# Fewer, larger transfers in a hybrid encoder layer on one core

## The chip, the core and the metric

The kernel runs on one core of a Trainium2 chip. Its time is the time on the device in microseconds (us), the median of several runs. A core has a matrix engine (TensorE, PE in the profile; its weight loads are PEld), VectorE (DVE), ScalarE (ACT), GpSimd (POOL) and SyncE (SP). Nearly every DMA of this kernel is issued from SP's queue, in one fixed order. An instruction of that queue that has to wait holds up all that stand behind it. 16 DMA engines carry the bytes.

## The reference

One layer works on two sequences, of 2048 and of 512 tokens, with 1024 channels:

```python
h = rms_norm(x, norm_w)
proj = h @ w_in                       # split into the inputs of four mixers
y_a = sgu(a_u, a_v) * silu(a_z)       # gating within chunks of 128 tokens
y_b = deltanet(b_q, b_k, b_v, b_beta, b_alpha) * silu(b_z)   # forward and backward
y_c = attention(c_q, c_k, c_v) * silu(c_z)   # 4 query heads, 2 key heads, QK norm, axial rope
y_d = pool(d_x) * silu(d_z)           # centred means of 2, 4, 8 and 16 tokens
y = x + concat(y_a, y_b, y_c, y_d) @ w_out
```

The DeltaNet is computed in chunks of 64 tokens: a unit lower triangular matrix of each chunk is inverted, and a recurrence carries a 64 x 64 state per head from chunk to chunk, once in each direction.

## The kernel before

The 2560 tokens are five blocks of 512 (`b`), or twenty tiles of 128 (`t`). Most matrix products run in fp16 on a high and a low part: three products stand for one in fp32.

- **Phase 1** (`phase1`, L200) loads x, normalises it, splits it into two halves in fp16 and stores the result `xs` to DRAM (L292, 2 MB a block). It computes the DeltaNet's q, k and v with their convolution (`conv`, L295, which stores keys and queries to `KX` and keys and values to `KV`) and the token-major inputs (`tmajor`).
- **Phase 2** (`phase2`, L564) runs three times, as three passes over other columns of `w_in`. For each block it loads `xs` again in eight pieces of 256 KB, one for each eighth `k` of the channels (`load_xs`, L737), into eight buffers. Each of the pass's products goes through `k` = 0 to 7 with three matmuls for each. A buffer comes free after the last product of the block has used its `k`. Weights arrive in columns of 128 (`split_w`, L101, and `weights`, L535): of each row of the weight matrix a piece of 512 B is read.
- **DeltaNet.** `pre(t)` (L1078) builds decay matrices and key products of one tile. It stores the four diagonal 32 x 32 blocks of every matrix to `DG`, once per direction (L1128), in pieces of 128 B, and the attention-like matrix to `AT` (L1132). A small product `ctp` with a copy `ct` (L1085 to L1090) prepares four tiles at once, when `t % 4 == 0`. `lanes` (L1135) loads the diagonal blocks of a whole block (L1145), inverts them on DVE and stores the inverses to `XL`. `levels(t)` (L1167) loads the inverses of two tiles in four transfers (L1179), joins them to inverses of 64 x 64 on PE, and stores these to `TT` (L1245). `rec(t, d, seq)` (L1256) is one step of the recurrence. It loads `kx`, `kv`, `at` and `tt`, 256 KB each (L1259 to L1265), into two buffers for each name. There are 40 such steps.
- **Phase 3** (`phase3`, L848) loads keys block by block (`load_kv`, L990: for one key head and block two transfers into `ka` and one into `kb`, 64 KB each), runs the attention with the row maxima one head ahead, and uses the output projection (`outproj`, L941) as filler on PE.

Inside `pre`, the tiles `ctp`, `gp` and `kk` take turns in the two PSUM banks of group `B` (four banks for the first block). Two allocations later the same bank is needed again, so it must have been read by then.

A planner (`schedule_with_timeline_sim`) orders each engine's instructions ahead of the run: by priorities (the DeltaNet's is above phase 2's, the attention's between) and by its own estimate of durations, transfers included. Other transfers can thus give another order on every engine.

Of the kernel before, what the change touches and what calls it, by code (L numbers as in the profile page):

```python
# [44 lines left out]
class Trunk:  # L45
# [55 lines left out]
    def split_w(self, pool, src, cols, tag, stage=None):  # L101
        nc = self.nc
        t = pool.tile([128, 2, 8, cols], F16, tag=tag, name=tag)
        for c in range(0, cols, 128):
            n = min(128, cols - c)
            w = self.stage() if stage is None else stage
            nc.sync.dma_start(w[:, :, :n], src[:, c:c + n].rearrange("(k p) c -> p k c", p=128))
            self.split_w_sb(t[:, :, :, c:c + n], w[:, :, :n])
        return t
# [13 lines left out]
    def mm_parts(self, ps, w, x):  # L123
        for k in range(8):
            for i, (a, b) in enumerate(((0, 0), (1, 0), (0, 1))):
                xk = x[k][:, b, :] if isinstance(x, list) else x[:, b, k, :]
                mm = self.nc.tensor.matmul(ps, w[:, a, k, :], xk, start=k + i == 0, stop=k == 7 and i == 2)  # L127
            yield mm.ins
# [11 lines left out]
    def consts(self, ctx):  # L140
# [8 lines left out]
        self.XS = [d.tile([128, 2, 8, 512], F16, name=f"xs{b}") for b in range(NB)]  # L149
        self.KX = [d.tile([4, 3, 64, 4, 2, 128], F16, name=f"kx{b}") for b in range(NB)]  # L150
        self.KV = [d.tile([4, 128, 512], F32, name=f"kv{b}") for b in range(NB)]
# [4 lines left out]
        self.AT = [[d.tile([128, 2, 512], F16, name=f"at{t}_{i}") for i in range(2)] for t in range(NT)]  # L156
        self.SZ = [[d.tile([128, 512], F32, name=f"sz{b}_{f}") for f in range(4)] for b in range(NB)]
        self.QS = [d.tile([2, 4, 64, 512], F16, name=f"qs{b}") for b in range(NB)]
        self.KS = [d.tile([2, 2, 64, 512], F16, name=f"ks{b}") for b in range(NB)]
        self.TT = [[d.tile([128, 2, 512], F16, name=f"tt{t}_{i}") for i in range(2)] for t in range(NT)]  # L160
# [39 lines left out]
    def phase1(self):  # L200
# [3 lines left out]
        with ExitStack() as ctx:  # L204
# [5 lines left out]
            def get_w(c, stage=None):  # L210
                if c not in W:
                    if c == "tm":
                        W[c] = self.split_w(wp, I["wtm"], 400, "wtm")
                    else:
                        W[c] = self.split_w(wp, I["wg1"][:, c * 128:(c + 1) * 128], 128, f"w1_{c}", stage)
                return W[c]
# [19 lines left out]
            def load_x(b):  # L236
# [47 lines left out]
                xs = (ho if b % 2 else he).tile([128, 2, 8, 512], F16, tag="xs", name="xs")  # L284
                for k in range(8):
                    stt = V.scalar_tensor_tensor(xt[k], xt[k], self.nw[:, k:k + 1], rb,
                                                 op0=ALU.mult, op1=ALU.mult)
                    act = A.activation(xs[:, 0, k, :], xt[k], AF.Copy)  # L288
                    if k == 3:
                        C["stt"], C["act"] = stt.ins, act.ins  # L290
                    (V if b == 0 and k % 2 else G).tensor_tensor(xs[:, 1, k, :], xt[k], xs[:, 0, k, :], op=ALU.subtract)  # L291
# [3 lines left out]
            def conv(b):  # L295
# [3 lines left out]
                for ct in range(6):  # L299
# [8 lines left out]
                    if ct < 4:  # L308
# [8 lines left out]
                        for par in range(2):  # L317
                            rows = slice(par * 64, par * 64 + 64)
                            for p in range(3):
                                nc.sync.dma_start(self.KX[b][:, p, :, par * 2 + pair, s, :].rearrange("t d f -> d t f"),  # L320
                                                  hl[rows, p % 2].rearrange("d (t f) -> d t f", t=4))
# [47 lines left out]
                nc.sync.dma_start(self.KV[b].rearrange("t p c -> p t c"), kv.rearrange("p t s h d -> p t (s h d)"))  # L369
# [18 lines left out]
            def tmajor(b, xs):  # L388
# [5 lines left out]
                for tt in range(4):  # L394
# [3 lines left out]
                    for k in range(8):  # L398
                        for a, c in ((0, 0), (0, 1), (1, 0)):
                            PE.matmul(acc[:, 0:400], xs[:, a, k, tt * 128:(tt + 1) * 128], w[:, c, k, :],  # L400
                                      start=n == 0, stop=n == 23)
                            n += 1
# [132 lines left out]
    def weights(self, *names):  # L535
# [8 lines left out]
        for n in names:  # L544
# [14 lines left out]
            if n in src:  # L559
                o, wd = src[n]  # L560
                nc.sync.dma_start(w[:, :, 0:wd], I["wg2"][:, o:o + wd].rearrange("(k p) c -> p k c", p=128))
            self.split_w_sb(self.W2[n], w)

    def phase2(self, names, ep, shared, stop=None):  # L564
# [117 lines left out]
        def store_qk(dst, s):  # L682

            if s.shape[2] == 2:
                for half in range(2):
                    for hl in range(2):
                        nc.sync.dma_start(dst[hl, :, half * 32:half * 32 + 32, :], s[:, hl, half, :])
            else:
                for half in range(2):
                    for hl in range(2):  # L690
                        nc.sync.dma_start(dst[hl, :, half * 32:half * 32 + 32, :], s[half * 64:half * 64 + 64, hl, 0, :])
# [27 lines left out]
        def finish_k(b, kt, rt):  # L719
# [6 lines left out]
            store_qk(self.KS[b], s)  # L726
# [121 lines left out]
    def phase3(self, kp, ap, wp, ep, e5, rest, post):  # L848
# [4 lines left out]
        if True:  # L853
# [136 lines left out]
            def load_kv(s0, n):  # L990
# [4 lines left out]
                for kv in range(2):  # L995
# [3 lines left out]
                    for b in range(n // 512):  # L999
                        kd = self.KS[s0 // 512 + b]  # L1000
                        c = slice(b * 512, b * 512 + 512)
                        for hl in range(2):
                            nc.sync.dma_start(ka[hl * 64:hl * 64 + 64, c], kd[hl, kv])
                        nc.sync.dma_start(kb[0:64, c], kd[0, kv])
# [63 lines left out]
    def front(self, dp, dq):  # L1068
# [9 lines left out]
        def pre(t):  # L1078
            grp = "B" if done else "B0"
            kx, ky = [dq.tile([128, 4, 2, 128], F16, tag=f"kx{i}", name="kx", bufs=2) for i in range(2)]  # L1080
            for i, x in enumerate((kx, ky)):
                nc.sync.dma_start(x.rearrange("p h s f -> p (h s f)"),
                                  self.KX[t // 4][t % 4, i:i + 2].rearrange("p d h s f -> (p d) (h s f)"))
            if t % 4 == 0:
                ctp = self.bank(grp, [128, 512], "ctp")  # L1085
                for i in range(4):
                    PE.matmul(ctp[0:24, i * 128:i * 128 + 128], self.C16[:, t + i].rearrange("p k c -> p (k c)"), self.id16,
                              start=True, stop=True)
                st["ct"] = dq.tile([24, 512], F16, tag="ct", name="ct", bufs=1)
                A.activation(st["ct"], ctp[0:24, :], AF.Copy)  # L1090
            ct = st["ct"][:, t % 4 * 128:t % 4 * 128 + 128]
# [14 lines left out]
            for par in range(2):  # L1106
# [6 lines left out]
                for d in range(2):  # L1113
# [3 lines left out]
                                           op0=ALU.mult, op1=ALU.mult)  # L1117
            for d in range(2):
                nl = nls[d]
                dg = dq.tile([128, 4, 32], F32, tag="dg", name="dg", bufs=2)  # L1120
                for B in range(4):
                    r = slice(B * 32, B * 32 + 32)
                    if d == 0:
                        V.transpose(dg[r], nl[r, :, r])
                    else:
                        A.activation(dg[r], nl[r, :, r], AF.Copy)
                l0 = (t % 4 * 2 + d) * 16
                nc.sync.dma_start(self.DG[t // 4][l0:l0 + 16].rearrange("(u b) (r c) -> (b r) u c", u=4, r=32), dg)  # L1128
# [3 lines left out]
                nc.sync.dma_start(self.AT[t][d], at)  # L1132
# [34 lines left out]
        def levels(t):  # L1167
# [5 lines left out]
            tnds = []  # L1173
            for d in both:
                TT, Tn = TTs[d], Tns[d]
                d32 = dp.tile([128, 8, 32], F32, tag=f"d32{d}", name="d32", bufs=1)
                for j in range(2):
                    l0 = ((t + j) % 4 * 2 + d) * 16
                    nc.sync.dma_start(d32[:, j * 4:j * 4 + 4], self.XL[t // 4][l0:l0 + 16].rearrange(  # L1179
                        "(u b) (c r) -> (b c) u r", u=4, c=32))  # L1180
# [57 lines left out]
            for d, Pr, Sr in ends:  # L1238
                TT = TTs[d]
                A.activation(TT[Pr, :, Sr], t2p[Pr], AF.Copy)  # L1240
                t16 = dp.tile([128, 2, 8, 128], F16, tag="tt16", name="tt16", bufs=1)
                A.activation(t16[:, 0], TT, AF.Copy)
                (G if d else V).tensor_tensor(t16[:, 1], TT, t16[:, 0], op=ALU.subtract)
                for j in range(2):
                    nc.sync.dma_start(self.TT[t + j][d], t16[:, :, j * 4:j * 4 + 4].rearrange("p i u f -> p i (u f)"))  # L1245
# [4 lines left out]
    def recurrence(self, dp):  # L1250
# [5 lines left out]
        def rec(t, d, seq):  # L1256
            b, tt = t // 4, t % 4
            kx = dp.tile([128, 4, 2, 128], F16, tag="kx3", name="kx3", bufs=2)
            nc.sync.dma_start(kx.rearrange("p h s f -> p (h s f)"),  # L1259
                              self.KX[b][tt, 0:2].rearrange("p d h s f -> (p d) (h s f)"))  # L1260
            kv = dp.tile([128, 2, 4, 64], F32, tag="kv2", name="kv2", bufs=2)
            nc.sync.dma_start(kv.rearrange("p s h d -> p (s h d)"), self.KV[b][tt])
            at, TT = [dp.tile([128, 2, 4, 128], F16, tag=n, name=n, bufs=2) for n in ("at2", "tt2")]
            nc.sync.dma_start(at.rearrange("p i u f -> p i (u f)"), self.AT[t][d])
            nc.sync.dma_start(TT.rearrange("p i u f -> p i (u f)"), self.TT[t][d])  # L1265
# [137 lines left out]
def host_arrays(np, inp):  # L1403
# [13 lines left out]
    out["wg1"] = np.concatenate([W["bq"][:, ph], W["bk"][:, ph], W["bv"][:, ph]], 1)  # L1417
    out["wtm"] = np.concatenate([W["av"], W["cv"], W["bb"], W["ba"]], 1)
# [20 lines left out]
    out["wg2"] = np.concatenate(cat, 1)  # L1439
# [46 lines left out]
```

## Time and profile before

| | us |
|---|---|
| median of 3 runs | 1571.06 (1570.57 to 1574.56) |
| the profiled execution | 1574.01 |
| its span | 1572.2 |
| PE busy | 1425.8 (91%) |
| DVE busy | 1173.3 (75%) |
| ACT busy | 797.0 (51%) |
| POOL busy | 546.7 (35%) |
| DMA, share of 16 engines | 54.1% |

The profile moves 269.65 MB in 250830 packets, 95784 of them under 512 B. Busy time of PE is the union of its instructions' times, and matmuls overlap; PE's granted clock was 0.959 of full speed in the mean. In a row of waits stand the engine and the line that waited, what it waited for, the sum in us, how often, and the longest. In a row of a timeline stand the start, the duration, the engine, the line, the instruction, how many, and in brackets the idle time before it with what ended it.

### The profile page before, as it was taken

Reading aid. Unit: us, or ns where it says so; the run is one execution under the profiler, and the core shown is the slowest. Engines: PE = TensorE matmul, PEld = TensorE weight load, DVE = VectorE, ACT = ScalarE, POOL = GpSimd, SP = SyncE. Lnnn points to the kernel's source line nnn. Section 1 sums busy time; section 2 is a strip of 40 time slices with the busy share of each in tenths; the row PEclk is TensorE's granted clock in tenths of the full one; section 3 lists DMA queues with packets and bytes.
Section 4 is the critical chain, followed back from the end, with each engine's and each line's share of the span. In section 5 each row is a group of like instructions: output and inputs, shape, how many; then the busy total and the mean of one; then the engine's idle time right before and its main releaser. Section 6 shows DMA issues by size and latency. Waiting matters only on the chain. (4 is left out here: it accounts for less than half of the span.)

```text
span 1572.2 us, 34743 instructions
## 1 busy us (share of the span) xinstructions
PE 1425.8 (91%) x13420; PEld 783.5 (50%) x13420; DVE 1173.3 (75%) x2265; ACT 797.0 (51%) x1655; POOL 546.7 (35%) x646
## 2 busy tenths in 40 slices
PE   6999999988989887987889879998799999999898
PEld 3456555543444443544445435555355555555443
DVE  6338579967969887996957769998877887877611
ACT  5244444545454844554546215565567675576400
POOL 3220220044748643455453435555121221121100
PEclk9999999998899989989999999999799999999999
DMA  9845643556566877657689885644411501414332
GB/s 254 283 168 168 190 151 114 150 194 193 160 186 201 258 234 218 199 171 215 186 259 311 278 255 177 202 139 148 161 48 39 173 34 65 160 33 135 114 128 107
DMA packets 250830, 269.65 MB, mean 172 GB/s; under 512 B 95784, under 2 KB 176680, under 8 KB 250024
## 3 DMA queue, kind: packets, MB, share of 16 engines
q1 hardware_dynamic: 250264, 267.36, 54.1%
q8 instruction: 105, 1.72, 0.4%
q14 instruction: 61, 0.50, 0.1%
q0 software_dynamic: 400, 0.07, 0.1%
HBM read 175.66 MB, written 91.77 MB: 170 GB/s over the span
## 5 line engine op out<-in xcount | busy, mean ns | idle before, releaser
L127 PEld LDWEIGHTS <-w 128*128 128x128 f16 x2280 | 223.5, 101 | 307.5 <-issue 81.8
L127 PE MATMUL accz<-xs,w 128*128 128x512 f16 x960 | 243.7, 402 | 16.8 <-DMA xs<-xs 6.7
L958 PE MATMUL op<-wo,mx 128*128 128x512 f16 x960 | 225.3, 379 | 1.0 <-DVE y L962 1.0
L886 DVE TENSOR_REDUCE mm<-mp 128x1 f32<-128x512 f32 x272 | 179.5, 683 | 52.4 <-PE mp L884 52.1
L916 POOL TENSOR_TENSOR p<-e,p 128x512 f16<-128x512 f32 x68 | 86.7, 1274 | 318.6 <-ACT p L915 283.7
L912 ACT ACTIVATE e<-sp 128x512 f32<-128x512 f32 x272 | 153.4, 596 | 79.3 <-PE sp L910 72.9
L916 DVE TENSOR_TENSOR p<-e,p 128x512 f16<-128x512 f32 x204 | 165.8, 828 | 19.3 <-ACT p L915 19.1
L127 PE MATMUL acc<-xs,w 128*128 128x512 f16 x720 | 162.8, 383 | 3.8 <-POOL xs L291 1.5
L915 ACT ACTIVATE p<-e 128x512 f16<-128x512 f32 x272 | 161.2, 632 | 3.4 <-PE O L921 2.0
L921 PEld LDWEIGHTS <-p 128*128 128x128 f16 x3264 | 128.1, 97 | 55.8 <-DVE p L916 11.2
L921 PE MATMUL O<-vt,p 128*128 128x65 f16 (+1 forms) x3264 | 142.6, 193 | 7.5 <-DVE p L916 5.3
L958 PEld LDWEIGHTS <-mx 128*128 128x128 f16 x960 | 91.3, 98 | 104.4 <-issue 1.8
L884 PE MATMUL mp<-ka,qa 128*128 128x512 f16 x272 | 98.7, 395 | 17.3 <-DVE mm L886 10.6
L909 PE MATMUL sp<-qa,ka 128*128 128x512 f16 x272 | 103.9, 384 | 2.6 <-ACT e L912 1.2
L306 DVE SCALAR_TENSOR_TENSOR cv<-raw,convw,cv 128x512 f32<-128x512 f32 x120 | 88.0, 754 | 21.2 <-POOL raw L382 20.6
L910 PE MATMUL sp<-qb,kb 65*128 65x512 f16 x272 | 100.5, 387 | 1.2 <-ACT qb L894 1.0
L127 PE MATMUL accq<-xs,w 128*128 128x512 f16 x360 | 89.5, 391 | 9.9 <-DMA xs<-xs 7.0
L400 PE MATMUL acct<-wtm,xs 128*128 128x400 f16 x480 | 83.8, 332 | 1.9 <-ACT ba L408 0.9
L1268 POOL TENSOR_TENSOR kd<-kv,kds 128x512 f16<-128x512 f32 x40 | 46.9, 1179 | 108.0 <-PE up L1305 56.0
L291 POOL TENSOR_TENSOR xs<-xt,xs 128x512 f16<-128x512 f32 x36 | 49.1, 1386 | 73.5 <-ACT xs L288 73.2
L962 DVE SCALAR_TENSOR_TENSOR y<-op,xr 128x512 f32<-128x512 f32 x40 | 27.5, 687 | 59.2 <-PE op L958 59.1
L127 PE MATMUL accu<-xs,w 128*128 128x512 f16 x240 | 60.9, 403 | 7.2 <-DVE s L616 7.0
(316 smaller groups left out, 2506.8 us busy)
## 6 DMA issues: line engine op xcount, KB each, us to landing
xs<-xs SPq DMA_DIRECT2D x120, 256.0 KB
kx<-kx SPq DMA_DIRECT2D x80, 256.0 KB
at<-at SPq DMA_DIRECT2D x80, 256.0 KB
tt<-tt SPq DMA_DIRECT2D x80, 256.0 KB
xt<-in_xT SPq DMA_DIRECT2D x40, 256.0 KB
xs<-xs SPq DMA_DIRECT2D x5, 2048.0 KB
kv<-kv SPq DMA_DIRECT2D x40, 256.0 KB
mix<-mixs SPq DMA_DIRECT2D x40, 256.0 KB
```

The source lines that it names most:

```text
L127: mm = self.nc.tensor.matmul(ps, w[:, a, k, :], xk, start=k + i == 0, stop=k == 7 and i == 2)
L306: V.scalar_tensor_tensor(cv, raw[:, ct, i:i + 512], self.convw[:, ct, i:i + 1], cv, op0=ALU.mult, op1=ALU.add)
L400: PE.matmul(acc[:, 0:400], xs[:, a, k, tt * 128:(tt + 1) * 128], w[:, c, k, :], start=n == 0, stop=n == 23)
L884: PE.matmul(mp, qa[:, qt * 128:qt * 128 + 128], KA[h // 2][:, sc * 512:sc * 512 + 512], start=True, stop=True)
L886: V.tensor_reduce(mm[:, qt, sc:sc + 1], mp, axis=AX.X, op=ALU.max)
L909: PE.matmul(sp, KA[kv][:, c], qa, start=True, stop=False)
L910: PE.matmul(sp, KB[kv][:, c], qb, start=False, stop=True)
L912: A.activation(e, sp, AF.Exp)
L915: A.activation(p[:, 0], e, AF.Copy)
L916: (G if st % E8 == 1 else V).tensor_tensor(p[:, 1], e, p[:, 0], op=ALU.subtract)
L921: mm = PE.matmul(O[:, qt, 0:z - a], p[:, w, q], v[:, a:z], start=st == 0 and qt == 0 and i == 0, stop=st == nst - 1 and i == 2, skip_group ...
L958: PE.matmul(op, mix[k][:, a, tt * 128:tt * 128 + 128], wo[k][:, c, n * 512:n * 512 + 512], start=i + j == 0, stop=i == 7 and j == 2)
```

## The change

- `xs` is stored with its halves beside each other for each `k`, and loaded in four pieces of 512 KB into four buffers (60 loads in place of 120).
- `KX` and `KV` become one tensor `KXV`, `AT` and `TT` one tensor `ATT`. A step of the recurrence loads two pieces of 512 KB in place of four of 256 KB.
- The diagonal blocks are stored once for two tiles and both directions (10 stores in place of 40), from one buffer in place of two. The inverses are loaded once for two tiles and both directions (10 in place of 40). `TT` is stored once per direction for two tiles (20 in place of 40).
- `ctp` and `ct` are made for each tile (20 in place of 5, each a quarter as wide).
- Keys are stored by sequence, and loaded in one transfer each for `ka` and `kb` (8 in place of 30).
- The host packs the weights so that a column block of 128 lies as 4 KB per partition.

```diff
+    def packed(self, w, src, o, n):
+        self.nc.sync.dma_start(w[:, :, :n], src[:, 8 * o:8 * (o + n)].rearrange("p (k c) -> p k c", k=8))
...
-            for k in range(8):
-                x = self.xp.tile([128, 2, 512], F16, tag="xs2", name="xs2", bufs=8)
-                nc.sync.dma_start(x, self.XS[b][:, :, k, :])
-                xs.append(x)
+            for k in range(0, 8, 2):
+                x = self.xp.tile([128, 2, 2, 512], F16, tag="xs2", name="xs2", bufs=4)
+                nc.sync.dma_start(x, self.XS[b][:, k:k + 2])
+                xs += [x[:, 0], x[:, 1]]
...
-                    for b in range(n // 512):
-                        kd = self.KS[s0 // 512 + b]
-                        c = slice(b * 512, b * 512 + 512)
-                        for hl in range(2):
-                            nc.sync.dma_start(ka[hl * 64:hl * 64 + 64, c], kd[hl, kv])
-                        nc.sync.dma_start(kb[0:64, c], kd[0, kv])
+                    kd = self.KS[self.seqs.index((s0, n))][kv]
+                    nc.sync.dma_start(ka, kd.rearrange("i d t -> (i d) t"))
+                    nc.sync.dma_start(kb[0:64], kd[0])
...
-            if t % 4 == 0:
-                ctp = self.bank(grp, [128, 512], "ctp")
-                for i in range(4):
-                    PE.matmul(ctp[0:24, i * 128:i * 128 + 128], self.C16[:, t + i]...
-                st["ct"] = dq.tile([24, 512], F16, tag="ct", name="ct", bufs=1)
-                A.activation(st["ct"], ctp[0:24, :], AF.Copy)
+            ctp = self.bank(grp, [128, 128], "ctp")
+            PE.matmul(ctp[0:24], self.C16[:, t].rearrange("p k c -> p (k c)"), self.id16, ...)
+            ct = dq.tile([24, 128], F16, tag="ct", name="ct", bufs=1)
+            A.activation(ct, ctp[0:24], AF.Copy)
...
+            if t % 2 == 0:
+                st["dg"] = dq.tile([128, 2, 2, 4, 32], F32, tag="dg", name="dg", bufs=1)
...
-                nc.sync.dma_start(self.DG[t // 4][l0:l0 + 16].rearrange(...), dg)
+            if t % 2:
+                l0 = t // 2 % 2 * 64
+                nc.sync.dma_start(self.DG[t // 4][l0:l0 + 64].rearrange(...), st["dg"]...)
...
-                for j in range(2):
-                    nc.sync.dma_start(d32[:, j * 4:j * 4 + 4], self.XL[t // 4][l0:l0 + 16]...
+            d32s = dp.tile([128, 2, 8, 32], F32, tag="d32", name="d32", bufs=1)
+            nc.sync.dma_start(d32s..., self.XL[t // 4][l0:l0 + 64]...)
...
-            nc.sync.dma_start(kx..., self.KX[b][tt, 0:2]...)
-            nc.sync.dma_start(kv..., self.KV[b][tt])
-            nc.sync.dma_start(at..., self.AT[t][d])
-            nc.sync.dma_start(TT..., self.TT[t][d])
+            kxv = dp.tile([128, 1024], F32, tag="kxv", name="kxv", bufs=2)
+            nc.sync.dma_start(kxv, self.KXV[b][tt, 0:128])
+            att = dp.tile([128, 2, 2, 4, 128], F16, tag="att", name="att", bufs=2)
+            nc.sync.dma_start(att..., self.ATT[t // 2][d][t % 2])
```

## Rows read from the trace of the kernel before

**Rows 1.** Windows by stretch: PE, PEld, DVE, ACT, POOL busy, PE clock, DMA share, GB/s.

```profile
320.00:480.00 160.00, 140.51 (x972) 68.68 (x969) 119.77 (x271) 84.53 (x217) 87.75 (x137) 0.90 0.58 179
480.00:640.00 160.00, 131.21 (x1442) 70.86 (x1440) 136.05 (x264) 89.43 (x213) 91.80 (x133) 0.91 0.73 225
640.00:800.00 160.00, 137.75 (x1695) 76.55 (x1696) 140.80 (x264) 82.80 (x184) 77.81 (x100) 0.91 0.66 199
800.00:960.00 160.00, 140.12 (x1622) 76.01 (x1621) 109.93 (x191) 60.93 (x121) 67.32 (x67) 0.96 0.85 271
960.00:1125.00 165.00, 145.01 (x1880) 87.07 (x1879) 147.50 (x269) 93.54 (x186) 82.21 (x79) 0.93 0.52 163
1125.00:1505.00 380.00, 368.87 (x3854) 209.39 (x3852) 289.34 (x507) 239.65 (x449) 74.88 (x56) 1.00 0.27 90
```

**Rows 2.** Waits of PE from 320 to 1120 us: sum, times, longest.

```profile
PE gp L1095 <- DVE dt L1116: 9.8, 6, 3.8
...
PE accq L127 <- DMA xs<-xs: 7.0, 8, 1.8
...
PE accz L127 <- DMA xs<-xs: 6.7, 6, 1.5
...
PE up L1300 <- DMA tt<-tt: 3.4, 2, 2.5
...
PE gp L1095 <- ACT ct L1090: 2.0, 1, 2.0
...
PE mp L884 <- DMA qa<-qs: 1.8, 1, 1.8
...
PE sp L909 <- DMA ka<-ks: 1.2, 1, 1.2
...
PE mp L884 <- DMA ka<-ks: 0.9, 1, 0.9
...
PE up L1300 <- DMA kb<-ks: 0.6, 1, 0.6
...
PE gp L1099 <- ACT ct L1090: 0.5, 1, 0.5
```

**Rows 3.** Timeline of SP's queue: the first and the last key load.

```profile
899.78 0.48 SPq L1003 DMA_DIRECT2D ka<-ks  x1
...
947.49 0.45 SPq L1004 DMA_DIRECT2D kb<-ks  x1
```

**Rows 4.** Timeline of PE in the same stretch.

```profile
907.01 4.05 PE L127 MATMUL accz<-xs,w 128*128 128x512 f16 x18
...
933.83 0.82 PE L127 MATMUL accz<-xs,w 128*128 128x512 f16 x3 [1.39 <-DMA xs<-xs]
935.96 1.41 PE L127 MATMUL accz<-xs,w 128*128 128x512 f16 x3 [1.31 <-DMA xs<-xs]
```

**Rows 5.** Issues on SP's queue by tile: duration in ns, least, median, most.

```profile
L741 SPq DMA_DIRECT2D xs<-xs x120: 517/562/2554, 47.9 to 1010.6; - x120
...
L1264 SPq DMA_DIRECT2D at<-at x40: 319/376/677, 356.8 to 1090.5; - x40
...
L1265 SPq DMA_DIRECT2D tt<-tt x40: 319/407/2168, 483.7 to 1084.2; - x40
...
L1179 SPq DMA_DIRECT2D d<-xl x40: 360/498/1196, 437.4 to 807.0; - x40
```

**Rows 6.** Windows around the first load of inverses, columns as in rows 1.

```profile
430.00:434.00 4.00, 3.88 (x10) 1.18 (x9) 1.83 (x6) 0.70 (x2) 2.04 (x12) 0.50 1.03 371
...
440.00:443.00 3.00, 3.00 (x15) 1.37 (x14) 0.00 (x0) 0.45 (x1) 1.16 (x1) 1.00 1.03 196
```

**Rows 7.** Waits of DVE for diagonal blocks and for inverses, whole span.

```profile
DVE ltmp L1153 <- DMA lnl<-dg: 20.2, 5, 7.2
...
DVE tnd L1183 <- DMA d<-xl: 10.2, 5, 4.5
```

**Rows 8.** Windows by stretch, the second 40 us, columns as in rows 1.

```profile
40.00:80.00 40.00, 37.86 (x199) 19.47 (x198) 15.93 (x33) 13.00 (x29) 10.61 (x9) 1.00 0.87 281
```

More of the change, by code (lines that the diff above doesn't have):

```diff
@@ L125, in mm_parts @@
             for i, (a, b) in enumerate(((0, 0), (1, 0), (0, 1))):
-                xk = x[k][:, b, :] if isinstance(x, list) else x[:, b, k, :]
-                mm = self.nc.tensor.matmul(ps, w[:, a, k, :], xk, start=k + i == 0, stop=k == 7 and i == 2)
+                xk = x[k] if isinstance(x, list) else x[:, k]
+                mm = self.nc.tensor.matmul(ps, w[:, a, k, :], xk[:, b, :], start=k + i == 0, stop=k == 7 and i == 2)
             yield mm.ins
@@ L148, in consts @@
         d = self.dram
-        self.XS = [d.tile([128, 2, 8, 512], F16, name=f"xs{b}") for b in range(NB)]
-        self.KX = [d.tile([4, 3, 64, 4, 2, 128], F16, name=f"kx{b}") for b in range(NB)]
-        self.KV = [d.tile([4, 128, 512], F32, name=f"kv{b}") for b in range(NB)]
+        self.XS = [d.tile([128, 8, 2, 512], F16, name=f"xs{b}") for b in range(NB)]
+        self.KXV = [d.tile([4, 192, 1024], F32, name=f"kxv{b}") for b in range(NB)]
         self.MIX = [[d.tile([128, 2, 512], F16, name=f"mix{b}_{f}") for f in range(8)] for b in range(NB)]
@@ L283, in load_x @@
                               self.ident, start=True, stop=True)
-                xs = (ho if b % 2 else he).tile([128, 2, 8, 512], F16, tag="xs", name="xs")
+                xs = (ho if b % 2 else he).tile([128, 8, 2, 512], F16, tag="xs", name="xs")
                 for k in range(8):
@@ L399, in tmajor @@
                         for a, c in ((0, 0), (0, 1), (1, 0)):
-                            PE.matmul(acc[:, 0:400], xs[:, a, k, tt * 128:(tt + 1) * 128], w[:, c, k, :],
+                            PE.matmul(acc[:, 0:400], xs[:, k, a, tt * 128:(tt + 1) * 128], w[:, c, k, :],
                                       start=n == 0, stop=n == 23)
@@ L682, in store_qk @@
         def store_qk(dst, s):
-            if s.shape[2] == 2:
-                for half in range(2):
-                    for hl in range(2):
[L687 to L691, printed above, removed]
+            for half in range(2):
+                for hl in range(2):
+                    nc.sync.dma_start(dst[hl, :, half * 32:half * 32 + 32, :], s[:, hl, half, :])
         def rope_q(a, c, cs):
@@ L725, in finish_k @@
             G.tensor_tensor(s[:, 1, 0], kt, s[:, 0, 0], op=ALU.subtract)
-            store_qk(self.KS[b], s)
+            i = sum(b * 512 >= s0 + n for s0, n in self.seqs)
+            c = b * 512 - self.seqs[i][0]
+            for half in range(2):
+                for hl in range(2):
+                    nc.sync.dma_start(self.KS[i][:, hl, half * 32:half * 32 + 32, c:c + 512], s[half * 64:half * 64 + 64, hl, 0, :])
         def later(ins):
@@ L1240, in levels @@
                 A.activation(TT[Pr, :, Sr], t2p[Pr], AF.Copy)
[L1241 to L1245, printed above, removed]
+                t16 = dp.tile([128, 2, 2, 512], F16, tag="tt16", name="tt16", bufs=1)
+                TTj = TT.rearrange("p (j u) f -> p j (u f)", j=2)
+                A.activation(t16[:, :, 0], TTj, AF.Copy)
+                (G if d else V).tensor_tensor(t16[:, :, 1], TTj, t16[:, :, 0], op=ALU.subtract)
+                nc.sync.dma_start(self.ATT[t // 2][d][:, :, 1].rearrange("j p c -> p j c"),
+                                  t16.rearrange("p j i f -> p j (i f)"))
         return pre, lanes, levels
@@ L1257, in rec @@
             b, tt = t // 4, t % 4
[L1258 to L1265, printed above, removed]
+            kxv = dp.tile([128, 1024], F32, tag="kxv", name="kxv", bufs=2)
+            nc.sync.dma_start(kxv, self.KXV[b][tt, 0:128])
+            kx = kxv.bitcast(F16)[:, 0:1024].rearrange("p (h s f) -> p h s f", h=4, s=2)
+            kv = kxv[:, 512:1024].rearrange("p (s h d) -> p s h d", s=2, h=4)
+            att = dp.tile([128, 2, 2, 4, 128], F16, tag="att", name="att", bufs=2)
+            nc.sync.dma_start(att.rearrange("p a i u f -> p a (i u f)"), self.ATT[t // 2][d][t % 2])
+            at, TT = att[:, 0], att[:, 1]
             kds = self.KDS[d][:, t, :].unsqueeze(2)
@@ L1416, in host_arrays, with packed @@
     out = {"x": x, "xT": x.T, "norm_w": g["norm_w"][0]}
-    out["wg1"] = np.concatenate([W["bq"][:, ph], W["bk"][:, ph], W["bv"][:, ph]], 1)
-    out["wtm"] = np.concatenate([W["av"], W["cv"], W["bb"], W["ba"]], 1)
+    def packed(w, widths):
+        o = np.cumsum([0] + widths)
+        return np.concatenate([w[:, a:b].reshape(8, 128, b - a).transpose(1, 0, 2).reshape(128, -1) for a, b in zip(o, o[1:])], 1)
+    out["wg1"] = packed(np.concatenate([W["bq"][:, ph], W["bk"][:, ph], W["bv"][:, ph]], 1), [128] * 6)
+    out["wtm"] = packed(np.concatenate([W["av"], W["cv"], W["bb"], W["ba"]], 1), [128, 128, 128, 16])
     cw = g["conv_w"][0]
@@ L1438, in host_arrays @@
     cat = [W["bz"], W["cq"][:, qx(0)], W["cq"][:, qx(1)], W["ck"][:, qx(0)[:64]], W["ck"][:, qx(1)[:64]], W["cz"], W["dz"], W["au"], W["az"]]
-    out["wg2"] = np.concatenate(cat, 1)
+    out["wg2"] = packed(np.concatenate(cat, 1), [64 if n in "CD" else 128 for n in Trunk.SRC])
     out["wdxT"] = W["dx"].T
```

55 lines of the change are left out of this document (27 added, 28 removed).

## The prediction, made before the result was known

> **What bounds the kernel now.** I read the windows by stretch first. The reader is to see two kernels in one. From 1125 us on, PE is busy for 368.87 of 380 us at a granted clock of 1.00, and the DMA engines are busy for 0.27 of the time: nothing about a transfer can be worth much there [rows 1]. From 320 to 960 us, where phase 2 and the DeltaNet run side by side, PE is busy for 140.51 + 131.21 + 137.75 + 140.12 = 549.6 of 640 us, so it idles for 90 us, its clock is granted at 0.90 to 0.96, and the DMA engines are busy for 0.58 to 0.85 of the time [rows 1]. The 40 us after the first 40 lose only 2.1 us [rows 8]. So the change can be paid in one currency, PE's idle time between 320 and 1120 us.
>
> Next the waits of PE in that stretch. Those that a transfer ended are 7.0 + 6.7 us for `xs`, 3.4 us for `tt`, 1.2 + 0.9 + 0.6 us for keys and 1.8 us for `qa`, together 21.6 us; the others end with DVE, ACT or POOL, such as 9.8 us in which `gp` waited for a bank that DVE had to read [rows 2]. Those others the change doesn't touch, except by the `ct` that it adds.
>
> Then the timeline of SP's queue and of PE between 899 and 948 us. In 48 us SP issues all 30 key loads, at 0.45 to 0.48 us each, so some 14 us of its queue, with loads of `xs` and of the recurrence in between [rows 3]; PE runs 18 matmuls in 4.05 us while its data is there, and stops for 1.39 and 1.31 us ahead of groups of three when an `xs` piece is late [rows 4]. This is the place where the transfers are the bound.
>
> **The change part by part.** The sum is made in PE time.
>
> *`xs` in four pieces.* 60 issues fewer at 0.562 us are 34 us of SP's queue [rows 5]. PE's waits for it are 13.7 us in 14 places [rows 2], at eight of the block starts. Against it: a pair comes free one `k` later, and a `k` is three matmuls at 4.05 / 18 = 0.225 us, so 0.68 us [rows 4]; and the first matmul waits for 256 KB more, 0.97 us at the 271 GB/s of 800 to 960 us [rows 1]. Bounds: all 13.7 us gained, or 8 x 1.65 = 13 us lost. I take 6 us gained, near half of the measured wait, because the late pieces stand in the stretch where SP's queue is full [rows 3], and this is what the change empties.
>
> *The recurrence with two loads.* 80 issues fewer at 0.376 to 0.407 us are about 31 us of SP's queue [rows 5]. The buffers stay at two for each, with the bytes the same. PE's waits for `tt` are 3.4 us [rows 2]: bounds 3.4 us gained and as much lost (a merged buffer is free only when the last user of both is done, and the next SP instruction stands behind that wait). I take 2 us gained.
>
> *Keys.* 22 issues fewer at about 0.46 us are 10 us of SP's queue in the 48 us in which it is full [rows 3]. PE's waits for keys are 2.7 us [rows 2]; against it, the first score product needs all 512 KB of `ka` in place of a piece of 64 KB, 1.7 us at 271 GB/s [rows 1], once. I take 2 us gained, between 2.7 gained and 1.7 lost.
>
> *Weights.* They load mostly in the first 80 us, of which the second half has 2.1 us of PE idle [rows 8]; the path of the first 20 us goes through x. Bounds 2.1 us gained and, as the bytes don't grow and nothing else moves there, nothing lost beyond as much again from another order. I take 1 us. The Trainium skill, page "DMA: Bandwidth & Descriptors", section "Specifications", gives 512 B as the smallest transfer at line rate; the weights' pieces are just that, so by it packing them wins nothing and the sum below would be 1 us smaller. No run here shows it yet.
>
> *`ctp` for each tile.* 15 more small products, 15 more copies on ACT, and one more turn of the two banks of `gp` and `kk`. Today five of them make PE wait 2.0 + 0.5 us in all [rows 2]. `gp` now takes the bank of the second `kk` in place of the first, so it waits for two more DVE reads, and behind a late `gp` stand PE's phase 2 matmuls. Bounds: nothing (the copy needs only constants, so it can run early), or 15 x 2.0 = 30 us. The nearest row is the average of 0.5 us, 15 x 0.5 = 7.5 us, and as three of today's five cost nothing I take 3 us lost.
>
> *Diagonal blocks and inverses by pairs.* The last store ahead of `lanes` has 2048 pieces of 128 B in place of 512, the load ahead of `levels` 2048 in place of the 1024 that the first direction needs. In full windows the rings move 371 GB/s, and 196 GB/s where the small pieces are [rows 6]: if the four loads (256 KB) all fell into those 3 us, the other 332 KB took 0.9 us and 2048 pieces about 2.1 us, my estimate. So a store is 1.6 us later, five times, and a load 1.05 us later, ten times, 18.5 us at most, all on DVE, which waits there 20.2 and 10.2 us today [rows 7]. Against that, three issues of 0.498 us fewer before each `levels` [rows 5], 15 us at most. DVE idles for 24 us of 160 in 480 to 640 [rows 1], and PE has phase 2 as filler: I take 1 us lost on PE, of -15 to +18.5. A single buffer for the blocks makes the next pair's transposes wait for the store; other DVE work between two tiles covers it, and without that cover it is part of the same bound.
>
> *Clock.* At 0.50 PE runs at 1.2 GHz, at 1.00 at 2.4 GHz [rows 6]. A mean of 0.90, 0.91, 0.91 and 0.96 is 2 x (1 - mean) of the time at the lower, 32 + 29 + 29 + 13 = 102 us [rows 1], which costs half of it, 51 us. Less idle time may give some back: 0 to 13 us (a quarter), I take 3.
>
> Sum: -6 - 2 - 2 - 1 + 3 + 1 - 3 = -10 us. The profiled execution took 1574.01 us (span 1572.2), 2.95 us above the median of the runs shown, so 1574.0 - 10 = 1564.0 there is 1561 us as a median. The planner will also set another order, which no row prices; I allow 8 us either way for it.
>
> **The rivals.**
> - *Hidden anyway* (1571 us): the bytes are the same, and PE's waits in the largest part, 90 - 21.6 = 68 us, end with other engines [rows 1, 2]. Against it: a queue as full as in rows 3 and 4 doesn't lose a quarter of its issues without effect.
> - *Coarser pieces* (1580 us): the block starts lose 13 us in place of winning 6, 1561 + 19. For it: PE reads eight pieces in sequence and needs only the first to start [rows 4]. Against: the engines are already up to 0.85 busy where the waits are [rows 1]. The Trainium skill's page "Perfetto Trace Analysis", section "DMA Optimizations", says the same as a rule: where DMA engines are mostly idle, smaller pieces may let work start sooner. The 0.27 after 1125 us would fit it, the 0.85 before doesn't.
> - *`ct` in PE's way* (1588 us, the slower side): every added copy holds `gp` as long as the longer of today's two did, 2.0 us, 30 us in place of 3. It decides from about 1.2 us each, 18 us, where the other gains of 13 us are eaten and 4.7 us (below) are lost. For it: 9.8 us already go to this pair of banks [rows 2]. Against: three of five copies cost nothing.
> - *The stretch closes up* (1538 us): all 19.8 us of waits for `xs`, `tt` and keys go and the clock gives back 13 us. For it: some 75 us of SP's queue are freed. Against: DVE at 136 and 141 of 160 us leaves PE other waits [rows 1].
>
> **How the numbers follow.** Forecast 0.40 (1552 to 1568), hidden 0.18, coarser 0.14, `ct` 0.14, closing up 0.14. A measurement of this kernel tells about 0.3%, 4.7 us, from no change. Faster is the forecast and the closing up, 0.54; the same is 0.18; slower is 0.28. The range 1538 to 1585 takes in the coarser pieces and leaves out most of the `ct` case and half of the closing up, about 0.2.
>
> **What would show it.** Right: waits of PE for `xs` near 8 us and for keys under 1 us, SP's issues between 880 and 950 us with gaps, PE's idle time from 320 to 960 us near 80 us. Wrong in a step: waits for `xs` of 20 us or more (coarser); waits of `gp` for `ct` of over 15 us; DVE's waits for `lnl` and `tnd` grown by more than 18 us. Wrong as a whole if PE's waits for transfers fall as said and the time stays, or if the stretch from 1125 us on changes by more than 5 us.

## The result: 0.5% slower, 8 us lost where 10 were forecast as won

| | before | changed |
|---|---|---|
| median, five runs each on one chip, us | 1574.56 | 1582.12 |
| ratio, 95% interval | | 1.0052 (1.0029 to 1.0075) |
| profiled execution, us | 1574.01 | 1579.81 |
| its span | 1572.2 | 1577.7 |
| PE busy | 1425.8 | 1420.4 |
| PE idle (span less busy) | 146.4 | 157.3 |
| DMA packets | 250830 | 188587 |
| DMA, share of 16 engines (first queue) | 54.1% | 52.7% |

The forecast was 1561 us. In the profiled executions PE works 5.4 us less and idles 10.9 us more; the difference, 5.5 us, is the longer span. The windows of the changed kernel, with the columns of [rows 1]:

```profile
320.00:480.00 160.00, 137.85 (x1071) 70.00 (x1066) 120.07 (x266) 86.89 (x229) 83.04 (x131) 0.90 0.57 182
480.00:640.00 160.00, 130.41 (x1299) 68.89 (x1298) 133.74 (x243) 84.65 (x202) 90.51 (x137) 0.92 0.68 208
640.00:800.00 160.00, 134.84 (x1768) 76.14 (x1766) 138.82 (x276) 82.88 (x190) 74.48 (x102) 0.91 0.66 205
800.00:960.00 160.00, 135.17 (x1590) 74.91 (x1590) 111.55 (x194) 69.22 (x135) 67.02 (x68) 0.94 0.78 255
960.00:1125.00 165.00, 147.43 (x1864) 88.36 (x1862) 146.73 (x269) 88.87 (x180) 83.67 (x80) 0.98 0.58 187
1125.00:1505.00 380.00, 364.27 (x3830) 207.56 (x3829) 290.18 (x506) 237.04 (x446) 74.76 (x56) 1.00 0.27 89
```

From 320 to 960 us PE is busy for 538.3 of 640 us, so it idles for 101.7 us, where [rows 1] gave 90.4 and I had forecast about 80. The loss lies where I had looked for the gain; from 1125 to 1505 us PE is busy 4.6 us less. PE's waits of the changed kernel (the sum, how often, the longest), answering to [rows 2]:

```profile
PE up L1303 <- DMA att<-att: 8.2, 2, 4.3
PE z1p L1209 <- DVE tnd L1186: 7.8, 3, 2.8
...
PE accz L131 <- DMA xs<-xs: 6.7, 2, 5.8
...
PE ctp L1085 <- DVE dt L1112: 5.3, 3, 4.2
...
PE gp L1091 <- DVE dt L1112: 3.8, 5, 1.2
...
PE gp L1091 <- ACT ct L1087: 3.6, 1, 3.6
...
PE accq L131 <- DMA xs<-xs: 2.3, 3, 1.2
...
PE gp L1095 <- ACT ct L1087: 0.9, 2, 0.6
...
PE mp L888 <- DMA ka<-ks: 0.3, 1, 0.3
```

The waits for `xs` fell from 13.7 to 9.0 us and those for keys from 2.7 to 0.3 us, nearly as forecast. Those for the step's merged tile rose from 3.4 us (`tt`) to 8.2 (`att`). All waits that a transfer ended fell from 22.4 to 18.2 us, those that POOL ended from 13.6 to 7.6, but those that DVE ended rose from 51.5 to 64.4 and those that ACT ended from 20.0 to 27.2, sums over all rows of this view. So the `xs` and key loads did what they should, the merged step load did not, and PE waited longer for other engines. This is near the case that I had named as wrong as a whole.

SP's queue, its first and last key load and what follows, answering to [rows 3] (start, duration):

```profile
895.14 0.49 SPq L1004 DMA_DIRECT2D ka<-ks  x1
...
910.85 0.45 SPq L1005 DMA_DIRECT2D kb<-ks  x1
...
918.26 0.32 SPq L1263 DMA_DIRECT2D kxv<-kxv  x1
923.72 0.32 SPq L1326 DMA_DIRECT2D od<-o  x1
924.09 0.42 SPq L1323 DMA_DIRECT2D ol<-od  x1
928.91 0.32 SPq L1403 DMA_DIRECT2D mix<-mixs  x1
```

The keys are issued within 16 us in place of 48, and the queue has the gaps that I forecast. DVE's waits for the diagonal blocks and the inverses, answering to [rows 7], grew by 2.4 us in all, not by the 18 us that would have marked that step wrong:

```profile
DVE ltmp L1156 <- DMA lnl<-dg: 24.1, 5, 6.6
...
DVE tnd L1186 <- DMA d<-xl: 8.7, 4, 4.4
```

### The profile page after: what moved, and what is told of

It is laid out like the page before. It is cut to its first block, busy times and chain, and to the rows that moved or that the text cites. A ratio compares the mean times of both kernels' runs of the same rounds, so it can differ in the third digit from the quotient of the medians.

```text
span 1577.7 us, 34295 instructions
## 1 busy us (share of the span) xinstructions
PE 1420.4 (90%) x13420; PEld 785.6 (50%) x13420; DVE 1175.3 (74%) x2265; ACT 798.0 (51%) x1670; POOL 539.6 (34%) x646
## 2 busy tenths in 40 slices
DMA packets 188587, 269.60 MB, mean 171 GB/s; under 512 B 91913, under 2 KB 108809, under 8 KB 187785
## 3 DMA queue, kind: packets, MB, share of 16 engines
q1 hardware_dynamic: 188024, 267.34, 52.7%
## 5 line engine op out<-in xcount | busy, mean ns | idle before, releaser
L131 PE MATMUL accz<-xs,w 128*128 128x512 f16 x960 | 236.6, 394 | 18.4 <-DMA xs<-xs 6.7
L1271 POOL TENSOR_TENSOR kd<-kxv,kds 128x512 f16<-128x512 f32 x40 | 43.6, 1090 | 155.7 <-PE up L1308 91.3
```

What stands on the lines that cost most here:

```text
L131: mm = self.nc.tensor.matmul(ps, w[:, a, k, :], xk[:, b, :], start=k + i == 0, stop=k == 7 and i == 2)
```

## The experiments

All were timed in five rounds beside the kernel before on the same chip. Every edit also makes the planner set another order on all engines. So several runs repeat a kernel in another order, by 20 memsets of 128 x 1 on DVE that are worth nothing in themselves. Where a theory was run in one order only, the text says so.

**The order by itself.** Into `pre` of the kernel before, and of the changed one:

```
+V.memset(dq.tile([128, 1], F32, tag="nil", name="nil", bufs=2), 0.0)
```

> The kernel before, with one 128x1 memset on DVE added to each of the 20 pre steps (under 0.1 us each, nobody reads it): it gives the planner another order and moves no data. Theory 1, the order: the change lost because the planner set another order on every engine, so an order that differs for no reason should differ in time as much as the change did, 0.3 to 1% in either direction. Theory 2, the transfers: the merged pieces themselves are late (inverses by pairs, merged step loads); then this kernel stays within 0.3% of before, ratio 0.997 to 1.003.

> The changed kernel with the same 20 small memsets on DVE. Theory 1: its time moves away from the changed kernel's 1.005 by 0.3% or more, to either side (0.995 to 1.015 against before). Theory 2: it stays at 1.003 to 1.008.

Measured: 0.9976 (0.9957 to 0.9995) and 0.9989 (0.9969 to 1.0009). The same work in another order moved one kernel by -0.24%, within the range of the second theory, and the other by -0.6%, outside it. An effect of one run below some 0.5% proves nothing here.

**The change in two halves.** First the pairs of blocks and inverses with `ctp` per tile, alone on the kernel before; then the changed kernel with just these two undone, so `xs`, steps, keys and weights merged:

```
 before                                   | changed kernel
+dg, d32 by pairs of tiles                | -dg, d32 by pairs of tiles
+ctp, ct for each tile                    | -ctp, ct for each tile
```

> The kernel before with only the diagonal blocks and inverses moved by pairs and ct made for each tile; xs, recurrence loads, keys and weights as before. Theory 2: this is where the loss is; DVE and PE wait for the later inverses, z1p waits for tnd by 5 us or more, time 1.004 to 1.010. Theory 1: no sign is foretold, anything from 0.993 to 1.010. Theory 3, the merged step loads cost: this stays at 0.998 to 1.002.

> The changed kernel with the pairs and ct undone: merged xs, step loads, keys and weights alone. Theory 2 (pairs lose): it is faster than before, 0.990 to 0.997, as the forecast's gains of 11 us stand alone. Theory 3 (merged step loads lose: PE waits for att 8 us): 1.003 to 1.010. Theory 1: anything from 0.990 to 1.010, and PE's waits for transfers lower than before while the other waits are spread over other engines.

Measured: 1.0037 (1.0019 to 1.0056) and 0.9928 (0.9902 to 0.9954), 1564.35 us. The second is faster than both kernels, and in the range that was named for a loss by these two; the first is just under its range. The same in another order:

> The change without pairs and without ct per tile, with a memset of 128 x 1 on DVE added in each step that builds a tile's decay matrices: 20 memsets of under 0.1 us, worth nothing in themselves, after which the planner sets another order on all engines. If the gain of 0.7% comes from the merged transfers: 0.990 to 0.996. If it was a lucky order: 0.997 to 1.003. The same memsets moved the kernel before by -0.24% and the changed one by -0.6%.

Measured: 0.9952 (0.9935 to 0.9970). So the merged loads and weights are worth 0.5 to 0.7% against the kernel before as it was; order for order, with that kernel at 1 and at 0.9976, it is 0.7 and 0.24%. Two windows, the changed kernel first, then the one without pairs and without `ct` per tile (columns as in [rows 1]).

```profile
800.00:1125.00 325.00, 282.60 (x3452) 163.27 (x3452) 258.28 (x462) 158.09 (x314) 150.69 (x147) 0.96 0.68 220
1125.00:1600.00 475.00, 432.69 (x4150) 238.89 (x4148) 302.69 (x524) 238.30 (x448) 74.76 (x56) 0.99 0.27 90
```

```profile
800.00:1125.00 325.00, 292.00 (x3343) 168.70 (x3340) 266.54 (x483) 162.94 (x314) 154.01 (x157) 0.97 0.66 217
1125.00:1600.00 475.00, 417.49 (x3933) 229.83 (x3930) 281.75 (x482) 224.05 (x420) 66.74 (x52) 0.99 0.26 86
```

After 1125 us PE is busy for at least 95% of the time in every run, so what counts is how much is left for PE by then: 3933 matmuls against 4150, 15.2 us of PE. The lead is older than these windows: by 800 us one kernel had done 6159 matmuls, the changed one 5825. The kernel before has 4143 left, and the three slowest kernels below 4325, 4251 and 4209.

**`ct` per tile, without pairs.**

```
 changed kernel:  -dg, d32 by pairs of tiles        (ctp, ct stay per tile)
```

> The changed kernel with the diagonal blocks and the inverses moved tile by tile and per direction again; everything else of the change stays, the product ctp and its copy per tile among it. Known: the whole change 1.0052 of before, the change without pairs and without ct per tile 0.9928. If ct per tile is the loss (its copy holds the bank of gp): 1.003 or more, and PE's waits of ctp and gp for DVE and ct stay at 13 us as in the changed kernel. If the pairs are the loss: 0.993 to 0.996, PE's waits there of some 13 us all the same, and the last store of the inverses some 40 us ahead of the changed kernel's 789 us. If it is the planner's other order alone: anything from 0.992 to 1.002, without a tie to either part.

> The run without pairs but with ct per tile, with the 20 memsets of 128 x 1 that change the planner's order. If ct per tile costs 1% whatever the order: 0.999 to 1.005 and the last store of the inverses at 780 us or later. If e5 was a bad draw: near 0.994 and before 765 us.

Measured: 1.0022 (1.0005 to 1.0039), and 0.9988 (0.9971 to 1.0004) in the other order. With `ct` per tile the gain is gone in both; the two ratios lie just beside the ranges that I had named for this, and far from those for the other parts. PE's largest waits of `ctp` and `gp` in the first, and then of the run with `ct` for four tiles:

```profile
PE gp L1095 <- ACT ct L1087: 10.3, 4, 8.0
...
PE ctp L1085 <- DVE dt L1112: 6.4, 4, 2.4
PE gp L1091 <- DVE dt L1112: 5.9, 5, 2.4
```

```profile
PE gp L1095 <- DVE dt L1116: 12.1, 5, 4.3
```

22.6 us against 12.1. The part that stands in the first row of the first is the one I had named for this rival, one wait of 8.0 us among it; in the other order it is 10.3 us as well. In the changed kernel it was 4.5 us.

**What of `ct` costs.** On the run with `ct` for four tiles, first only the turn of the banks with a product and a copy that nobody needs, then only a copy that `gp` needs:

```
+cu = self.bank(grp, [128, 128], "ctu"); PE.matmul(cu[0:24], C16[:, t], id16)
+A.activation(nobody's tile, cu[0:24], AF.Copy)
---
-ct = st["ct"][:, quarter of t]
+ct = dq.tile([24, 128]); A.activation(ct, st["ct"][:, quarter of t], AF.Copy)
```

> The change without pairs, with ct made for four tiles at once as before; added is, for each tile, the small product into a bank of the group of gp and kk and its copy on ACT to a tile that nobody reads. So the banks turn as with ct per tile, but gp waits for no new copy beyond the bank's. Known: without it 0.9928 and 0.9952 (two orders), last store of the inverses at 750 and 756 us; with ct per tile 1.0022 and 794 us. If the turn of the banks is what costs: 0.999 or more and the last store at 780 us or later. If it is the copy that gp needs: 0.993 to 0.996, last store before 765 us. If only the planner's draw of an order: no tie, anything from 0.992 to 1.004.

> The change without pairs, with ct made for four tiles at once as before; added is, for each tile, a copy on ACT of its quarter of ct (24 x 128, from SBUF to one buffer), which gp then reads. No product and no bank is added, but each gp has the copy ahead of it, and the copy waits for the gp of the tile before. If the copy in the chain of gp is what costs: 0.999 or more and the last store of the inverses at 780 us or later. If it is the turn of the banks: 0.993 to 0.996, last store before 765 us. If only the planner's draw: no tie.

Measured: 0.9941 (0.9922 to 0.9960) and 0.9931 (0.9905 to 0.9956). Neither costs anything alone, each in one order. They also end a theory of mine: the last store of the inverses, which I had taken as what sets the time, is at 785 and 802 us in these two, as late as in the slower kernels. Then `ct` per tile with `ctp` in a bank apart from those of `gp` and `kk`, without and with the pairs:

```
-ctp = self.bank(grp, [128, 128], "ctp")
+ctp = self.bank("C", [128, 128], "ctp")
```

> The same without the pairs of diagonal blocks and inverses: ct per tile, ctp in the bank of group C. If the chain bank, ctp, copy, gp is the cost: 0.993 to 0.996, as in the four orders with ct for four tiles. If ct per tile costs through its copies and products however they are placed: 0.999 to 1.002, as in the two orders with ctp in gp's banks. Difference to c1 is the price of the pairs, which I take as under 0.2%.

> The changed kernel with one thing changed: ctp takes its turn in the bank of group C in place of those of gp and kk. It is still made and copied for each tile. If ct per tile costs because ctp waits for a bank that DVE still reads and gp then waits for the copy: 0.993 to 0.998, PE's waits of ctp and gp for DVE, ACT and ct down from 16.6 us to some 11 us. If the loss is the planner's draw or the pairs: 0.999 to 1.005 as in the two orders of the changed kernel (1.0052, 0.9989).

Measured: 0.9976 (0.9955 to 0.9997) without pairs and 1.0141 (1.0114 to 1.0168) with them. The waits went as the theory said; of the run without pairs:

```profile
PE gp L1091 <- DVE dt L1112: 3.5, 5, 1.2
...
PE ctp L1085 <- DVE dt L1112: 1.9, 1, 1.9
...
PE gp L1095 <- ACT ct L1087: 0.9, 2, 0.6
```

6.3 us in these rows in place of 22.6, but the ratio fell by 0.46% against the one order with `ct` in those banks and by 0.12% against the other, 7 and 2 us, and it stayed between the two ranges I had given. So PE's waits for `ct` are the price in part at best. And with the pairs this kernel is the slowest of all, outside every range that I had named for it.

**`ct` per tile on the kernel before.**

```
 before:  +ctp, ct for each tile
```

> The kernel before with one part of the change alone: ctp and ct per tile. If ct per tile costs by itself: 1.002 to 1.010, PE's waits of ctp and gp for DVE and ct above 11.8 us (9.8 and 2.0 in the kernel before). If it costs only where the merged transfers had let the front end sooner: 0.998 to 1.002, with the last store of the inverses near the 789 us of before, since that kernel's front is as late as those with ct per tile already.

Measured: 1.0041 (1.0023 to 1.0058). It costs there too, but PE's waits of `gp` for `ct` and for DVE's reads of `kk` are 0.8 + 1.4 us in place of 2.5 + 9.8, so the place that I gave is not where it is paid.

**The pairs apart: the stores, and the merged load.** First `ct` per tile and stores by pairs, with four loads; then the fast kernel with the merged load alone:

```
 changed kernel:              -d32 in one load
 without pairs, without ct:   +d32 in one load
```

> As the run without pairs, with the diagonal blocks stored by pairs of tiles and both directions (one store of 256 KB, one buffer), and the inverses still loaded in four transfers. If the store by pairs is the loss (the first tile's blocks wait for the second tile, a single buffer, 2048 pieces of 128 B ahead of the inversion): 1.003 or more and DVE's waits for the blocks (lnl) near 24 us. If the merged load is: 0.993 to 0.997, and DVE's waits for the blocks near 20 us. If ct per tile is: 1.003 or more, and the run without pairs is there too.

> The change without pairs and without ct per tile (0.9928 of before), with one thing added: the inverses of two tiles and both directions come in one load in place of four. If the merged load is the loss (the first direction waits for the bytes of both): 1.000 or more, the sum of DVE's waits for d32 (tnd) grown by some 10 us (1 us at each of ten places) against the run without it, where it is 17 us. If the load is harmless: 0.990 to 0.996. If it is the planner's order alone: anywhere from 0.990 to 1.002, with the waits for d32 unchanged.

Measured: 1.0125 (1.0102 to 1.0148) and 0.9972 (0.9953 to 0.9992). The stores by pairs cost 1.0% against the run without pairs, the load 0.2 to 0.4% against the two orders without it, between the ranges that I had named (DVE's waits for the inverses grew by 4.3 us, not by 10). Four comparisons with the same rest stand now for pairs: +1.0% (stores only), +0.3% (the changed kernel), 0.0% (in the other order) and +1.65% (with `ctp` apart). I had taken them as under 0.2%. Where the price is largest, DVE's waits show it; with pairs and then without:

```profile
DVE ltmp L1156 <- DMA lnl<-dg: 36.1, 5, 10.7
...
DVE tnd L1186 <- DMA d<-xl: 19.3, 6, 5.9
```

```profile
DVE ltmp L1149 <- DMA lnl<-dg: 17.7, 4, 7.3
...
DVE tnd L1179 <- DMA d<-xl: 8.2, 4, 5.8
```

55.4 us against 25.9: DVE idles 29.5 us more ahead of the inversions and levels, the last store of the inverses is at 866.5 us for 822.0, and the time is 25 us longer. Elsewhere this sum doesn't follow the price: with the stores by pairs, 1.0% slower, it is 36.1 us for 39.0 without them; in the changed kernel 32.8 us; and in the run with the added copy, 0.9931, it is 40.6 us. So it explains one case of four.

**The merges one by one, on the kernel before.**

```
 c3: +xs2 = [128, 2, 2, 512], four loads   | c4, d1: +kxv, att, two loads a step
 d2: +packed weights, +one load each for ka and kb
     (c4, d1: and one store of tt for two tiles)
```

> The kernel before with the xs loads alone merged: four pieces of 512 KB in place of eight. By the prediction's term -6 us: 0.996, with PE's waits for xs at about 8 us in place of 13.7. If the coarser pieces cost: 1.002 or more and waits for xs of 20 us or more. The order draws of this kernel spread by some 0.25% either way, so 0.994 to 0.999 is taken as agreeing.

> The kernel before with the loads of a step of the recurrence alone merged: two of 512 KB in place of four of 256 KB (and the store of tt for two tiles). By the prediction's term -2 us: 0.999, PE's waits for tt and att near 3 us. If the merged tile comes later than tt alone did: PE's waits for att of 6 us or more (8.2 in the changed kernel) and 1.001 or more.

> The run with the steps' loads merged alone, with the 20 memsets of 128 x 1 that change the planner's order. If merging these loads costs by itself: 1.006 or more again. If the 1.0105 was one order: 0.996 to 1.002.

> The kernel before with packed weights and merged key loads alone, its order the same until the keys. By the prediction's terms -1 and -2 us: 0.998, the first 320 us 1 us of PE ahead, PE's waits for keys under 1 us. If these two carry the gain of 0.6%: 0.996 or less. If the order's later part draws badly: above 1.000 with the first 800 us the same as before.

Measured: `xs` 0.9999 (0.9979 to 1.0018), steps 1.0105 (1.0081 to 1.0129) and 1.0111 (1.0083 to 1.0138) in the other order, weights and keys 0.9947 (0.9927 to 0.9967). The last leaves the order on DVE the same for 1407 of its 2265 instructions, so it is the cleanest of all, though in one order only: up to 800 us PE is busy for 709.1 us as before (709.2), then for 289.1 us of 325 in place of 285.1. The exponentials of the attention and its key loads (duration in ns, then the first and the last start), here and then in the kernel before:

```profile
L915 ACT ACTIVATE e<-sp x272: 575/597/643, 939.0 to 1480.8; 128x512 f32<-128x512 f32 x136
...
L1003 SPq DMA_DIRECT2D ka<-ks x4: 319/374/491, 894.0 to 907.2; - x4
```

```profile
L912 ACT ACTIVATE e<-sp x272: 573/597/633, 948.7 to 1489.5; 128x512 f32<-128x512 f32 x136
...
L1003 SPq DMA_DIRECT2D ka<-ks x20: 444/472/795, 899.8 to 946.8; - x20
```

The attention starts 9.7 us sooner and ends 8.7 us sooner, as the span does (1563.6 for 1572.2). But the first key load is itself 5.8 us sooner. Up to it SP's queue holds the same 1331 instructions in the same order, so what stands ahead of it isn't won by the key loads. The first `accz` product of phase 2 starts at 314.8 us for 317.3, the last store of the inverses at 784.4 for 789.2. Between, DVE, still in the same order, is 1.3 us ahead at 517 us and 4.7 at 567; PE's order differs from 467 us on. What the key loads themselves did shows from 890 to 960 us: PE's waits for `xs` there fall from 6.4 us (4.2 of them behind the first key load) to none and those for keys from 2.7 to none, and PE is busy for 62.7 us of 70 in place of 58.5. Of this 3 us are left at the end, 8.6 less 5.8.

The steps' merge shows on SP's queue. Its loads of `kxv` wait for DVE to have read the buffer; in the kernel before the loads of `kv` waited 17.7 us for that, and those of `kx` 9.4 us for PE. Waits of SP with the steps merged alone:

```profile
SPq L1259 <- DVE r L1295: 44.2, 16, 9.8
SPq L1263 <- PE up L1311: 33.1, 16, 6.1
SPq L1127 <- DVE dg L1123: 30.9, 15, 4.4
```

And with everything merged but pairs and `ct`, the fast kernel:

```profile
SPq L1260 <- DVE r L1296: 56.0, 22, 8.7
SPq L1264 <- PE up L1312: 44.3, 15, 7.8
```

The wait is longer still in the fast one, so it is not in itself the loss. Nor did PE's waits for `att` show the sign that I had named, 6 us or more: they are 3.9 us and, in the other order, none. PE's longest waits differ between the two orders: 17.9 us for the recurrence's state `S` (1.1 in the kernel before), and 20.3 us of `gp` for `dt` (9.8). Alone the three parts give -0.01%, +1.08% and -0.53%, together -0.5 to -0.7%: they don't add. Why the steps' merge loses alone and not beside the others stays open; the fast kernel with the steps unmerged wasn't run.

## Why the prediction was wrong, by its steps

Built up from the kernel before, each kernel in the order first planned and in the one with the 20 memsets (1575 us for a ratio of 1; the last two columns are each row less the row above it):

| | first order | other order | mean, us | forecast |
|---|---|---|---|---|
| kernel before | 1 | 0.9976 | | |
| `xs`, steps, keys, weights | 0.9928 | 0.9952 | -7.6 | -11, and -3 for the clock |
| `ct` per tile on top | 1.0022 | 0.9988 | +10.2 | +3 |
| pairs on top: the changed kernel | 1.0052 | 0.9989 | +2.4 | +1 |

- **The step that failed** is the term *`ctp` for each tile*, forecast as 3 us lost and measured as 14.8 us in the first order and 5.7 in the other. It alone eats what the merges win. All three runs with `ct` per tile (the third, with `ctp` in a bank apart, 0.9976) lie above all four with `ct` made for four tiles at once (0.9928 to 0.9952). The price is inside the bounds of 0 to 30; I took it from what the waits for `ct` cost in the kernel before, and the runs show that the waits of `gp` are only a part. I had also written that the change doesn't touch the waits for other engines, and those for DVE and ACT grew by 20 us. The rival *`ct` in PE's way* comes nearest to what happened, at under half its price, and its sign, over 15 us of waits of `gp` for `ct`, didn't come (4.5 us). What passes the loss on is not settled: neither turn nor copy costs alone, and taking `ctp` out of the banks gave back 7 or 2 us, in one order.
- **The pairs** cost 4.7 and 0.2 us in the change itself, but 16 us with stores alone and 26 with `ctp` apart, the last beyond my upper bound of 18.5. All four are single pairs of runs in which the order changes too, so no price can be given. I argued that "other DVE work between two tiles covers" the single buffer; that was not tested. Where the price is largest, the waits that grew are those for the loads of the blocks and of the inverses, the other part of my bound.
- **Keys and weights**, forecast -3, gave -8.3 in one order. Some 2.5 us stand at the start of phase 2, just beyond the weights' bound of 2.1, and 3 us come behind the first key load, near the 2.7 us of waits by which I had bounded the keys. The rest came between, where neither acts directly and PE's order differs; that it is the order is not shown.
- **`xs`**, forecast -6, gave nothing measurable alone, though PE's waits for it fell from 13.7 to 5.9 us there, in a profiled execution that was itself 8 us under the median of its kernel. PE's waits that DVE ended rose from 51.5 to 62.1 us. The sign for coarser pieces, 20 us of waits for `xs`, didn't come in the changed kernel either (9.0).
- **Steps**, forecast -2 within 3.4 either way, gave +17 alone in two orders. My sentence that "a merged buffer is free only when the last user of both is done" fits SP's waits; bounding its price by PE's 3.4 us of waits for `tt` was wrong. What passes the 17 us on is open.
- **Luck.** The sum of the merges came out at -7.6 for -11 though alone its parts gave 0, +17 and -8: the agreement is luck and bears out no term.
- **Clock**, forecast -3. PE's busy time fell by 5.4 us at a mean granted clock of 0.962 for 0.959 in the profiled execution, but that is the highest of the changed kernel's five, which are 0.956 in the mean, and 0.954 in the other order; the kernel before had 0.960 over 30 executions. So the clock gave nothing back.
- **Order.** Two orders of the changed kernel differ by 0.63%, 10 us from end to end, for which I had allowed 8 us either way. Part of the 1.0052 is this: in the other order the changed kernel is level with the one before. That it isn't 10 us faster holds in both.
- **Weights.** In the first 40 us the rings moved 282 GB/s at a share of 0.89 with packed weights; before it was 250 at 0.90, and 251 at 0.91 with `xs` alone merged. The Trainium skill, page "DMA: Bandwidth & Descriptors", section "Specifications", has 512 B as enough for the line rate, by which pieces of 4 KB should move no more. The trace doesn't agree: at nearly the same share 13% more bytes went through. The packets of these 40 us say the same: those of 512 B took 32 ns in the mean in the kernel before, those of 4 KB 184 ns with packed weights, eight times the bytes in under six times the time.

## What to carry to other kernels

A wait for a transfer doesn't say what caused it: PE's waits for `xs` around 900 us went when the key loads that stood ahead of them on the same queue were merged. Before a gain is put down to one part, find the last instruction up to which both kernels have the same order and compare the times there: two thirds of the gain of keys and weights were there ahead of the first key load. A merged buffer waits for the later of its readers, so test each merge alone and beside the rest. In a kernel that a planner orders anew at every edit, run each finding in a second order before it is believed.

## What the runs showed that I had not expected

Where the waits of the whole kernel look the same, the count of matmuls left at the start of the last, full stretch tells the faster kernels from the slower: 3933 left at 0.9928, 4143 for the kernel before, 4325 at 1.0141. Between kernels within some 0.5% of each other it doesn't. An issue on SP took 0.32 us at its least. The `xs` issues, halved in number and with twice the bytes each, fell from a median of 0.562 us [rows 5] to 0.382:

```profile
L745 SPq DMA_DIRECT2D xs<-xs x60: 319/382/3371, 44.0 to 1043.4; - x60
```
